# Gate and up products of six SwiGLU layers by Strassen's seven products, with two weight sums formed by DMA

## The chip, the cores and the metric

The kernel runs on one core of a Trainium2 chip, in one launch. The metric is the device time of one execution in microseconds (us). The core has TensorE (PE, with its weight loads listed apart as PEld), VectorE (DVE), ScalarE (ACT), GpSimd (POOL) and SyncE (SP), each with an instruction queue of its own, and 16 DMA engines that move data between HBM and the on-chip memory (SBUF). TensorE writes its results into PSUM.

## The reference

Two models of 512 tokens and width 1,024 run one behind the other, two layers each, in float32, with six SwiGLU feed-forward parts (FFN) of inner width 2,816:

```python
def first_block(x, ...):                     # twice (l = 0, 1)
    ...                                      # four kinds of attention, then y
    x = _layernorm(ALPHA * x + y, ln1_g[l], ln1_b[l])
    f = (jax.nn.silu(x @ w_gate[l]) * (x @ w_up[l])) @ w_down[l]
    x = _layernorm(ALPHA * x + f, ln2_g[l], ln2_b[l])

def swiglu(h, w_gate, w_up, w_down):
    return (jax.nn.silu(h @ w_gate) * (h @ w_up)) @ w_down

def second_block(x, ...):                    # twice (l = 0, 1)
    x = x + 0.5 * swiglu(rms_norm(x, ffn_norm[l, 0]), ...)
    ...                                      # sparse attention, RWKV, gated delta rule
    x = x + 0.5 * swiglu(rms_norm(x, ffn_norm[l, 1]), ...)
```

The six FFNs are called FFN1 to FFN6 here, in the order in which they run: FFN1 and FFN2 belong to the first model, FFN3 (layer 0, first), FFN4 (layer 0, second), FFN5 and FFN6 to the second.

## The kernel before

Activations lie transposed: eight tiles `x[k]` of 128 channels by 512 tokens. Every matrix product is computed to nearly float32 accuracy from halves: an operand is cast to a rounded part `h` (ACT) and the rest `l` is a subtraction (DVE), and one product is three matmuls, h·h, h·l and l·h, which add up in PSUM (`mm3`, which calls `mm`, L164).

An FFN works on 22 "f tiles" of 128 of the 2,816 inner columns. For one f tile, gate and up take 2 (gate, up) x 8 (k tiles) x 3 = 48 matmuls with 512 columns of tokens. Their weights come by `weight` (L222 and after): one DMA of 128x1024 (512 KB) on SP's queue into a raw tile (tag "wr", three of them), the cast `gh` or `uh` on ACT (L235), and the subtraction `gl` or `ul` on DVE (L236), into tags "wh" and "wl" (three each). The result is taken out of PSUM by silu on ACT (L592, L595) and a multiplication on DVE (`hh`, L597), and split into `hh` and `hl` (L213, L214). Where the input is normalised by rms (FFN3 to FFN6), a factor `rs` per token is multiplied in afterwards (L594 and L599), so the products run on un-normalised tiles.

The 22 f tiles are worked in two halves of 11 (`HALF`): gate and up of 11 f tiles, then the down product of these 11 (eight output tiles of 33 matmuls with 512 columns, weights in pieces of 768 and 640 columns), then the same for the other 11. The down result is added into `x[j]` by DVE (`evac`, given by the caller).

Where an FFN follows a layer norm (FFN1, FFN2, FFN3), its first three (`PRE1`, FFN1 and FFN2) or four (`PRE2`, FFN3) f tiles are "early": their products are taken on the not yet normalised `x` (`presplit`, `psh` and `psl`) with 256-column matmuls `gup` and 258-column matmuls `gux` (`gemmx`, L343), while DVE and ACT work through the layer norm (`ln`, L506 to L520). ACT and DVE copy the results out (`gr`, `ur`, `gw`), and `unfold` (L477 to L479) puts the norm in later.

A tile framework with a scheduler orders the instructions of each engine from their priorities and inserts the semaphores; within one engine the order is then fixed. PSUM has eight banks in tags "s" (four), "o" and "d" (two each).

## Time and profile before

| | |
|---|---|
| time before, median of 3 runs | 3742.06 us (3739.53 to 3742.39) |
| the profiled execution's own time | 3745.34 us |
| its span, first to last instruction | 3743.6 us |
| mean granted TensorE clock | 0.985 |
| busy: PE, PEld, DVE, ACT, POOL | 97 %, 78 %, 56 %, 39 %, 8 % |
| HBM traffic over the span | 85 GB/s |

The profile is one execution. Busy time of PE is the sum of its matmuls as the trace shows them; these are pipelined, so one that lasts 0.39 us is followed by the next one 0.23 us later. How fast a row of matmuls runs is therefore read from start to start ("pitch"), not from the mean duration; the same holds in a smaller measure for DVE and ACT.

### The profile page before, as it was taken

Reading aid. Unit: us, or ns where it says so; the run is one execution under the profiler, and the core shown is the slowest. Engines: PE = TensorE matmul, PEld = TensorE weight load, DVE = VectorE, ACT = ScalarE, POOL = GpSimd, SP = SyncE. Lnnn points to the kernel's source line nnn. Section 1 sums busy time; section 2 is a strip of 40 time slices with the busy share of each in tenths; the row PEclk is TensorE's granted clock in tenths of the full one; section 3 lists DMA queues with packets and bytes.
Section 4 is the critical chain, followed back from the end, with each engine's and each line's share of the span. In section 5 each row is a group of like instructions: output and inputs, shape, how many; then the busy total and the mean of one; then the engine's idle time right before and its main releaser. Section 6 shows DMA issues by size and latency. Waiting matters only on the chain.

```text
span 3743.6 us, 48619 instructions
## 1 busy us (share of the span) xinstructions
PE 3644.6 (97%) x18628; PEld 2936.3 (78%) x18628; DVE 2103.4 (56%) x4405; ACT 1443.8 (39%) x2706; POOL 289.8 (8%) x294
## 2 busy tenths in 40 slices
PE   9999999899999999999998999999999999799999
PEld 7678888776788888888786878888888777688887
DVE  5378334637753357345799564444444678865343
ACT  5455222546442235223443542233223433543222
POOL 1111000111200000001212000000000211100000
PEclk9999999999999999999998999999999999899999
DMA  3113232221223222324212132323233321213232
GB/s 129 47 60 101 85 103 88 92 67 49 89 89 103 87 93 89 103 88 142 81 56 64 40 105 86 101 89 102 84 103 100 95 70 50 80 38 104 92 98 87
DMA packets 146840, 320.67 MB, mean 86 GB/s; under 512 B 31496, under 2 KB 57768, under 8 KB 146352
## 3 DMA queue, kind: packets, MB, share of 16 engines
q1 hardware_dynamic: 146608, 317.57, 26.8%
...
## 4 chain that ended last, share of the span: by engine, by line
PE 88%; DVE 9%; ACT 1%; issue 1%; DMA 1%; POOL 0%; DVEq 0%; ACTq 0%; POOLq 0%
PE gup L164 37%; PE dn L164 19%; PE pjp L164 7%; PE wop L164 4%; PE tp L164 3%; PE sc L164 2%; PE ot L164 1%; PE pt L168 1%; PE gux L164 1%; PE iY L164 1%; PE iR L164 1%; PE G L164 1%; PE rowp L164 1%; PE sb L164 1%; DVE isc L1775 1%
## 5 line engine op out<-in xcount | busy, mean ns | idle before, releaser
L164 PE MATMUL dn<-hh,downl 128*128 128x512 f32 x1056 | 416.2, 394 | 0.0
L164 PE MATMUL dn<-hh,downh 128*128 128x512 f32 x1056 | 416.0, 394 | 0.0
L164 PE MATMUL dn<-hl,downh 128*128 128x512 f32 x1056 | 415.8, 394 | 0.0
L164 PE MATMUL gup<-xsh,gh 128*128 128x512 f32 x976 | 384.7, 394 | 0.6 <-ACT xsh L216 0.6
L164 PE MATMUL gup<-xsl,gh 128*128 128x512 f32 x976 | 384.8, 394 | 0.0
L164 PE MATMUL gup<-xsh,gl 128*128 128x512 f32 x976 | 384.5, 394 | 0.0
L164 PE MATMUL gup<-xsh,ul 128*128 128x512 f32 x976 | 384.5, 394 | 0.0
L164 PE MATMUL gup<-xsh,uh 128*128 128x512 f32 x976 | 384.3, 394 | 0.0
L164 PE MATMUL gup<-xsl,uh 128*128 128x512 f32 x976 | 384.1, 394 | 0.0
L235 ACT CAST downh<-down 128x768 fp32r<-128x768 f32 x192 | 150.1, 782 | 517.9 <-PE dn L164 318.6
L597 DVE TENSOR_TENSOR hh<-gup,silu 128x512 f32<-128x512 f32 x122 | 84.4, 692 | 398.0 <-PE gup L164 392.5
L235 ACT CAST gh<-g 128x1024 fp32r<-128x1024 f32 (+1 forms) x138 | 139.3, 1014 | 412.2 <-issue 324.9
L236 DVE TENSOR_TENSOR downl<-down,downh 128x768 fp32r<-128x768 f32 x192 | 171.8, 895 | 216.7 <-ACT downh L235 216.7
L235 ACT CAST uh<-u 128x1024 fp32r<-128x1024 f32 (+1 forms) x138 | 139.5, 1014 | 353.6 <-PE gup L164 313.7
L236 DVE TENSOR_TENSOR ul<-u,uh 128x1024 fp32r<-128x1024 f32 (+1 forms) x138 | 162.4, 1178 | 151.4 <-ACT uh L235 149.4
L164 PEld LDWEIGHTS dn<-hl,downh 128*128 128x128 f32 x1056 | 198.3, 188 | 46.7
L164 PEld LDWEIGHTS dn<-hh,downl 128*128 128x128 f32 x1056 | 198.3, 188 | 46.6
L164 PEld LDWEIGHTS dn<-hh,downh 128*128 128x128 f32 x1056 | 198.3, 188 | 46.4
L164 PEld LDWEIGHTS gup<-xsh,gh 128*128 128x128 f32 x976 | 183.2, 188 | 44.2 <-ACT xsh L216 1.9
L164 PEld LDWEIGHTS gup<-xsl,gh 128*128 128x128 f32 x976 | 183.2, 188 | 43.6 <-DVE xsl L520 0.6
L164 PEld LDWEIGHTS gup<-xsl,uh 128*128 128x128 f32 x976 | 183.2, 188 | 43.0
L164 PEld LDWEIGHTS gup<-xsh,ul 128*128 128x128 f32 x976 | 183.3, 188 | 42.7
(595 smaller groups left out, 7411.2 us busy)
## 6 DMA issues: line engine op xcount, KB each, us to landing
g<-in_w_gu_dram SPq DMA_DIRECT2D x132, 512.0 KB, 3.5
u<-in_w_gu_dram SPq DMA_DIRECT2D x132, 512.0 KB, 3.5
...
pj<-in_w_in_dram SPq DMA_DIRECT2D x62, 512.0 KB, 3.6
...
wo<-in_w_o_dram SPq DMA_DIRECT2D x96, 128.0 KB, 2.2
xd<-x SPq DMA_DIRECT2D x24, 256.0 KB, 2.0
x<-xd SPq DMA_DIRECT2D x24, 256.0 KB, 4.7
```

The source lines that it names most:

```text
L164: self.nc.tensor.matmul(out, l, r, start=start, stop=stop)
L168: self.nc.tensor.transpose(out, src, self.ident if ident is None else ident)
L235: nc.scalar.copy(hi, r)
L236: (eng or nc.vector).tensor_sub(lo, r, hi.bitcast(F32))
L597: nc.vector.tensor_mul(hh, u, s)
L1775: nc.vector.match_replace(acc, m8, acc, -2.0 * BIG)
```

## The change

For f tiles 4 to 21 of every FFN (18 of 22, nine pairs), gate and up are no longer computed as 48 matmuls of 512 columns for each f tile. The two f tiles of a pair are stacked, and the product is seen as a 2x2 by 2x2 block product: gate and up are the two rows, the two halves of the 1,024 channels the inner index (blocks a, b of gate; c, d of up), and the two halves of 256 tokens the columns. Strassen's method, in the form with few additions, computes this from seven block products instead of eight. Each of the seven is 2 (f tiles) x 4 (k tiles) x 3 = 24 matmuls with 256 columns.

The weights of the seven are a, e = c+d, e+a, b, a+c, e+b (with e already holding c+d+a) and d, each split anew into h and l (ACT cast L646, DVE subtraction L647 of the changed kernel). Two of the sums are made by the DMA engines: POOL issues a DMA that adds a block from HBM onto a tile in SBUF (`accum_op`, L621), for e = c+d and for a+c; two are additions on DVE (L640, L642). A pair so takes six DMAs of 512 KB, and the seven products' results are put together by copies on ACT and additions on DVE that read PSUM. Weights are prepared two products ahead (`SAHEAD`), in five raw tiles (`NRAW`) and one of the old ones for b.

The sums of the tokens' side are made once for each FFN (`combos`): for each of four k, seven DVE operations of 256 columns and two of 512, three ACT operations of 256 and two casts of 512, and two more ACT operations where a gain is multiplied in.

The FFN is worked in three chunks (`CHUNKS`): gate and up of f tiles 4 to 11 and their down product, then 12 to 15 with the first four, then 16 to 21. The first four f tiles are now early ones in FFN1 to FFN3 (`PRE1` goes from 3 to 4), and direct 512-column ones in FFN4 to FFN6 (`PRE0`); all are copied out raw, and their silu, split and norm (`later`) run during the first down product. The down weights are repacked: 24 DMAs of 1,024 or 768 columns for an FFN instead of 32, and x is added to 24 times instead of 16. Quarter and half tiles of the mixing part now share their place in SBUF with the raw weight tiles (`phase`), and `presplit` makes its two small copies on ACT (L481, L482) instead of another engine.

```diff
-HALF = 11
+CHUNKS = ((4, 5, 6, 7, 8, 9, 10, 11), (12, 13, 14, 15, 0, 1, 2, 3), (16, 17, 18, 19, 20, 21))
+NRAW = 5
+SAHEAD = 2
 BIG = 1.0e30
 ALPHA = 4.0 ** 0.25
 SLOT = 520
 NWR = 3
 NWS = 3
 HEAD = 1
-PRE1 = 3
+PRE1 = 4
 PRE2 = 4
+PRE0 = 4
...
+    def combos(self, x, gcol, out):
...
+        for k in range(KT // 2):
+            p, q = x[k], x[k + KT // 2]
+            if gcol is not None:
+                g = []
+                for j, v in ((k, p), (k + KT // 2, q)):
+                    g.append(self.S("xg"))
+                    nc.scalar.activation(g[-1], v, AF.Copy, scale=gcol[:, j:j + 1])
+                p, q = g
+            nh, nl, g = self.S("cnh", F32R), self.S("cnl", F32R), self.S("cg", F32R)
+            t, u = self.S("ct"), self.S("cu")
+            nc.scalar.activation(nh[:, A], p[:, A], AF.Copy, scale=-1.0)
+            nc.scalar.activation(nh[:, B], q[:, B], AF.Copy, scale=-1.0)
+            nc.scalar.copy(g[:, A], q[:, A])
+            nc.vector.tensor_sub(t[:, A], p[:, B], p[:, A])
+            nc.vector.tensor_sub(t[:, B], q[:, B], t[:, A])
+            yield
+            nc.vector.tensor_sub(u[:, A], p[:, B], q[:, B])
+            nc.vector.tensor_sub(u[:, B], q[:, A], t[:, B])
+            hl = []
+            for v in (t, u):
+                hl.append((self.S("cth", F32R), self.S("ctl", F32R)))
+                nc.scalar.copy(hl[-1][0], v)
+            for v, r in ((p, A), (q, B)):
+                nc.vector.scalar_tensor_tensor(nl[:, r], v[:, r], -1.0, nh[:, r].bitcast(F32), op0=OP.mult, op1=OP.subtract)
+            nc.vector.tensor_sub(g[:, B], q[:, A], g[:, A].bitcast(F32))
+            for v, (h, l) in zip((t, u), hl):
+                nc.vector.tensor_sub(l, v, h.bitcast(F32))
+            for m, (h, l) in enumerate(((nh[:, A], nl[:, A]), (hl[0][0][:, A], hl[0][1][:, A]), (hl[0][0][:, B], hl[0][1][:, B]),
+                                        (g[:, A], g[:, B]), (hl[1][0][:, A], hl[1][1][:, A]), (nh[:, B], nl[:, B]),
+                                        (hl[1][0][:, B], hl[1][1][:, B]))):
+                out[m].append((h, l))
+            yield
...
+        def move(i, q, t, add=False):
+            g, h = quarter[q]
+            f = f0 + 2 * i
+            src = wgu[g, f:f + 2, :, h * 512:h * 512 + 512].rearrange("f p c -> p f c")
+            if add:
+                nc.gpsimd.dma_start(t.rearrange("p (f c) -> p f c", f=2), src, accum_op=OP.add)
+            else:
+                nc.sync.dma_start(t.rearrange("p (f c) -> p f c", f=2), src)
...
+        def prep(j):
+            i, s = divmod(j, 7)
+            R = lambda q: raws[i, q]
+            if s == 0:
+                if i == 0:
+                    load(0, "e", "c")
+                    move(0, "d", R("e"), True)
+                    load(0, "a")
+                load(i, "d")
+                load(i, "b")
+            elif s == 2:
+                nc.vector.tensor_add(R("e"), R("e"), R("a"))
+            elif s == 5:
+                nc.vector.tensor_add(R("e"), R("e"), R("b"))
+                del raws[i, "b"]
+            r = R("aeebaed"[s])
+            hi, lo = (tile_(self.wp, "w" + t, NWS, F32R) for t in "hl")
+            nc.scalar.copy(hi, r)
+            nc.vector.tensor_sub(lo, r, hi.bitcast(F32))
+            ws[j] = hi, lo
+            if s == 2:
+                move(i, "c", R("a"), True)
+            if s == 4 and i + 1 < n // 2:
+                load(i + 1, "e", "c")
+                move(i + 1, "d", raws[i + 1, "e"], True)
+                load(i + 1, "a")
+            if s >= 4:
+                del raws[i, "aed"[s - 4]]
...
+        for j in range(total):
+            i, s = divmod(j, 7)
+            if j + SAHEAD < total:
+                prep(j + SAHEAD)
+            between(j)
...
+            for e in range(2):
+                for k in range(H):
+                    w = slice(e * 512 + k * 128, e * 512 + k * 128 + 128)
+                    x, first, last = cs[s][k], fresh and k == 0, k == H - 1
+                    self.mm(a[e], hi[:, w], x[0], first, False, not fresh)
+                    self.mm(a[e], hi[:, w], x[1], False, False, not fresh)
+                    self.mm(a[e], lo[:, w], x[0], False, last, not fresh)
+            A, B = slice(0, 256), slice(256, 512)
+            for e in range(2):
+                if s == 0:
+                    g[e] = self.S("gt")
+                    nc.scalar.copy(g[e][:, A], a[e])
+                elif s == 1:
+                    if e == 0:
+                        u = self.S("up")
+                        u2 = {0: u[:, A], 1: u[:, B]}
+                    nc.scalar.copy(u2[e], a[e])
+                elif s == 2:
+                    nc.scalar.copy(g[e][:, B], a[e])
+                elif s == 3:
+                    nc.vector.tensor_sub(g[e][:, A], a[e], g[e][:, A])
+                elif s == 4:
+                    nc.vector.tensor_add(u2[e], a[e], u2[e])
+                elif s == 5:
+                    nc.vector.scalar_tensor_tensor(g[e][:, B], a[e], -1.0, g[e][:, B], op0=OP.mult, op1=OP.subtract)
+                    if rows() is not None:
+                        nc.vector.tensor_mul(g[e], g[e], rows())
+                    nc.scalar.activation(g[e], g[e], AF.Silu)
+                else:
+                    put(f0 + 2 * i + e, g[e], a[e], u2[e])
...
+        def put(f, s, ua, ub):
+            nc.vector.tensor_mul(s[:, 0:256], ua, s[:, 0:256])
+            nc.vector.tensor_mul(s[:, 256:512], ub, s[:, 256:512])
+            if stats is not None:
+                nc.vector.tensor_mul(s, s, rows)
+            h[f] = self.split(s, "h")
...
-                    gu = raw.pop(0)
+            if finish:
+                raw.append(early(f, xs))
+                if f == 1:
+                    lnr = rows
+                    todo = finish(lnr, cs)
+            else:
+                raw.append([(self.evac(ps, "a", name="gu"[i] + "r"), None) for i, ps in enumerate(products(f, xs))])
...
+            new = [f for f in fs if f >= npre]
+            self.fast(wgu, new[0], len(new), cs, lambda: rows if stats is not None else None, put, between)
+            last = n == len(CHUNKS) - 1
+            if last:
+                self.phase("M")
+                cs = None
             for j in range(KT):
-                if half and ahead and j == KT - 3:
+                if last and ahead and j == KT - 3:
                     ahead()
                 acc = self.P("dn", "do"[j % 2])
-                for a, b in ((0, 6), (6, HALF)):
-                    w = self.weight(wdn[half, j, :, a * 128:b * 128], b - a, 128, "down")
-                    for f in range(a, b):
-                        self.mm3(acc, w[f - a], h[o + f], f == 0, f == HALF - 1)
-                evac(half, j, acc)
+                w = self.weight(wdn[j, :, o * 128:(o + len(fs)) * 128], len(fs), 128, "down")
+                for i, f in enumerate(fs):
+                    self.mm3(acc, w[i], h[f], i == 0, i == len(fs) - 1)
+                evac(n == 0, last, j, acc)
+                if n == 0:
+                    next(rest, None)
+            for f in fs:
+                h[f] = None
+            o += len(fs)
 
 
```

Three places show how the order of instructions moves. The first is DVE in FFN1, where the layer norm ends. Before, its last additions (L506, L507) and the subtractions `xsl` that the direct products read (L520) stand among the early tiles' multiplications (L477, `ur`) and the weights' splits (L236):

```order
L506 TENSOR_TENSOR lnt_858_3499<-x_512_2030,lnr_813_3204 128x512
L520 TENSOR_TENSOR xsl_844_3375<-x_510_2026,xsh_843_3374 128x512
L507 TENSOR_TENSOR lnt_858_3499<-lnt_858_3499,lnb_814_3205 128x512 [waits DVE_49]
L506 TENSOR_TENSOR lnt_861_3507<-x_513_2032,lnr_813_3204 128x512
L236 TENSOR_TENSOR gl_883_3606<-g_881_3603,gh_882_3605 128x1024 [waits DMAHW5_49,Activation_49]
L507 TENSOR_TENSOR lnt_861_3507<-lnt_861_3507,lnb_814_3205 128x512 [waits DVE_49]
L520 TENSOR_TENSOR xsl_860_3504<-x_511_2028,xsh_859_3503 128x512 [waits Activation_49]
L506 TENSOR_TENSOR lnt_864_3515<-x_514_2034,lnr_813_3204 128x512
L520 TENSOR_TENSOR xsl_863_3512<-x_512_2030,xsh_862_3511 128x512 [waits Activation_49]
L507 TENSOR_TENSOR lnt_864_3515<-lnt_864_3515,lnb_814_3205 128x512 [waits DVE_49]
L477 TENSOR_TENSOR ur_856_3494<-ur_856_3494,lnr_813_3204 128x512
```

Now the layer norm is over before these rows; `gw` (L369) copies from the PSUM tile `gux` of the fourth early f tile, `ur` (L492) is that tile's multiplication, and the rows L584 to L597 are `combos` of the first k, with the split of the third product's weights (`swwl`, L647) among them:

```order
L492 TENSOR_TENSOR gr_857_3554<-gr_857_3554,lnr_815_3211 128x512
L369 COPY gw_861_3609<-gux_859_3559 128x2 [waits Activation_49]
L492 TENSOR_TENSOR ur_860_3608<-ur_860_3608,lnr_815_3211 128x512
L584 TENSOR_TENSOR ct_865_3616<-x_508_2023 128x256
L587 TENSOR_TENSOR cu_866_3617<-x_508_2023,x_512_2031 128x256
L585 TENSOR_TENSOR ct_865_3616<-x_512_2031,ct_865_3616 128x256 [waits DVE_49]
L595 TENSOR_TENSOR cg_864_3615<-x_512_2031,cg_864_3615 128x256 [waits Activation_49]
L588 TENSOR_TENSOR cu_866_3617<-x_512_2031,ct_865_3616 128x256 [waits DVE_49]
L647 TENSOR_TENSOR swwl_907_3724<-swwr2_898_3705,swwh_906_3723 128x1024 [waits Activation_49]
L594 SCALAR_TENSOR_TENSOR cnl_863_3614<-x_508_2023,cnh_862_3613 128x256
L594 SCALAR_TENSOR_TENSOR cnl_863_3614<-x_512_2031,cnh_862_3613 128x256
L597 TENSOR_TENSOR ctl_868_3626<-ct_865_3616,cth_867_3625 128x512 [waits Activation_49]
```

So the whole of `combos`, four groups like this, now stands behind a copy of the last early tile, where before there was no such sum. The second place is PE at the same point of FFN1. Before, direct products of 512 columns follow the last early matmul there. Now the last early matmul is followed by the first two of the seven products, on `cnh`, `cnl`, `cth`, `ctl` from `combos`, and these two are taken in turn k by k:

```order
L179 MATMUL gux_859_3559<-psh_794_3049,ul_844_3379 128x258
L179 MATMUL gup_908_3728<-cnh_862_3613,swwh_902_3714 128x256 [waits Activation_49]
L179 MATMUL gup_909_3729<-cnh_862_3613,swwh_902_3714 128x256
L179 MATMUL gup_914_3762<-cth_867_3625,swwh_904_3718 128x256 [waits Activation_49]
L179 MATMUL gup_915_3763<-cth_867_3625,swwh_904_3718 128x256
L179 MATMUL gup_908_3728<-cnl_863_3614,swwh_902_3714 128x256 [waits DVE_49]
L179 MATMUL gup_908_3728<-cnh_862_3613,swwl_903_3715 128x256
L179 MATMUL gup_909_3729<-cnl_863_3614,swwh_902_3714 128x256
L179 MATMUL gup_909_3729<-cnh_862_3613,swwl_903_3715 128x256
L179 MATMUL gup_914_3762<-ctl_868_3626,swwh_904_3718 128x256 [waits DVE_49]
```

Each k of the first two products waits for its own sums. The third place is DVE in the middle of gate and up in an FFN with rms factors. Before, one f tile is these six rows:

```order
L594 TENSOR_TENSOR silu_4240_19527<-gup_4238_19477,rs_4179_19165 128x512 [waits PE_49]
L236 TENSOR_TENSOR ul_4249_19546<-u_4247_19543,uh_4248_19545 128x1024 [waits DMAHW5_49,Activation_49]
L597 TENSOR_TENSOR hh_4241_19530<-gup_4239_19478,silu_4240_19527 128x512 [waits PE_49,Activation_49]
L599 TENSOR_TENSOR hh_4241_19530<-hh_4241_19530,rs_4179_19165 128x512 [waits DVE_49]
L236 TENSOR_TENSOR gl_4258_19612<-g_4256_19609,gh_4257_19611 128x1024 [waits DMAHW6_49,Activation_49]
L214 TENSOR_TENSOR hl_4243_19534<-hh_4241_19530,hh_4242_19533 128x512 [waits Activation_49]
```

Now this stands at the border of two pairs in FFN6 (`gt` and `up` hold the pair's gate and up, `swwr2_6971` is e of the next pair, `swwr_6980` its b):

```order
L647 TENSOR_TENSOR swwl_6984_36402<-swwr2_6971_36269,swwh_6983_36401 128x1024 [waits DMASW7_49,Activation_49]
L761 TENSOR_TENSOR gt_6962_36228<-gup_6960_36202,gt_6962_36228 128x256 [waits PE_49,Activation_49]
L762 TENSOR_TENSOR gt_6962_36228<-up_6968_36262,gt_6962_36228 128x256
L761 TENSOR_TENSOR gt_6963_36230<-gup_6961_36203,gt_6963_36230 128x256 [waits PE_49,Activation_49]
L764 TENSOR_TENSOR gt_6962_36228<-gt_6962_36228,rs_6607_33833 128x512 [waits DVE_49]
L762 TENSOR_TENSOR gt_6963_36230<-up_6968_36262,gt_6963_36230 128x256
L640 TENSOR_TENSOR swwr2_6971_36269<-swwr2_6971_36269,swwr2_6972_36272 128x1024
L229 TENSOR_TENSOR hl_6986_36433<-gt_6962_36228,hh_6985_36432 128x512 [waits Activation_49]
L764 TENSOR_TENSOR gt_6963_36230<-gt_6963_36230,rs_6607_33833 128x512 [waits DVE_49]
L647 TENSOR_TENSOR swwl_6990_36445<-swwr2_6971_36269,swwh_6989_36444 128x1024 [waits Activation_49]
```

The sum e+a (L640) and the split of it (the `swwl` that reads `swwr2_6971` again) stand behind five of the finished pair's operations. On POOL's queue, which had no DMA at this place, stand the adding DMAs, two for each pair; in FFN1 (`swwr2_899` is a of the first pair, `swwr2_950` e of the third pair):

```order
L621 DMA swwr2_899_3708<-in_w_gu1_dram 128x2x512 [waits DVE_49,Activation_49]
L621 DMA swwr2_950_4038<-in_w_gu1_dram 128x2x512 [waits DMAHW7_49,DMASW0_49,DVE_49]
L621 DMA swwr2_920_3798<-in_w_gu1_dram 128x2x512 [waits DMAHW2_49,DVE_49,Activation_49]
L621 DMA swwr2_981_4281<-in_w_gu1_dram 128x2x512 [waits DMAHW3_49,DMASW1_49,DVE_49]
```

The first of these waits for DVE (the sum e+a) and ACT (the cast of a) before it may add c onto a.

## Rows read from the trace of the kernel before

**Rows 1.** the page's head and its busy time by engine (us, share, instructions)

```profile
span 3743.6 us, 48619 instructions
PE 3644.6 (97%) x18628; PEld 2936.3 (78%) x18628; DVE 2103.4 (56%) x4405; ACT 1443.8 (39%) x2706; POOL 289.8 (8%) x294
```

**Rows 2.** the page's chain that ended last, by engine and by line

```profile
PE 88%; DVE 9%; ACT 1%; issue 1%; DMA 1%; POOL 0%; DVEq 0%; ACTq 0%; POOLq 0%
PE gup L164 37%; PE dn L164 19%; PE pjp L164 7%; PE wop L164 4%; PE tp L164 3%; PE sc L164 2%; PE ot L164 1%; PE pt L168 1%; PE gux L164 1%; PE iY L164 1%; PE iR L164 1%; PE G L164 1%; PE rowp L164 1%; PE sb L164 1%; DVE isc L1775 1%
```

**Rows 3.** the page's costliest groups: line, engine, operation, shapes, count, busy us, mean ns, idle

```profile
L164 PE MATMUL gup<-xsh,gh 128*128 128x512 f32 x976 | 384.7, 394 | 0.6 <-ACT xsh L216 0.6
...
L164 PEld LDWEIGHTS gup<-xsh,gh 128*128 128x128 f32 x976 | 183.2, 188 | 44.2 <-ACT xsh L216 1.9
```

**Rows 4.** windows in the first and fifth FFN: us, busy per engine, granted clock, DMA share, GB/s

```profile
496.08:618.46 122.38, 122.38 (x528) 98.90 (x527) 39.74 (x43) 33.73 (x43) 0.00 (x0) 1.00 0.30 92
...
2604.00:2664.00 60.00, 60.00 (x262) 48.94 (x261) 27.11 (x32) 17.87 (x22) 0.00 (x0) 1.00 0.29 90
```

**Rows 5.** timeline of PE in the first FFN, direct products: start, duration

```profile
379.99 0.39 PE L164 MATMUL gup<-xsh,gh 128*128 128x512 f32 x1
...
383.00 0.40 PE L164 MATMUL gup<-xsl,gh 128*128 128x512 f32 x1
```

**Rows 6.** timeline of PE in the early tiles of the first FFN

```profile
309.58 0.28 PE L164 MATMUL gux<-psl,gh 128*128 128x258 f32 x1
...
311.48 0.29 PE L164 MATMUL gux<-psh,gl 128*128 128x258 f32 x1
```

**Rows 7.** the same timeline, 6 us earlier, after an idle of PE

```profile
303.02 0.39 PE L164 MATMUL gup<-psl,gh 128*128 128x256 f32 x1 [0.64 <-DVE psl L469]
...
304.34 0.42 PE L164 MATMUL gux<-psl,uh 128*128 128x258 f32 x1
...
306.90 0.41 PE L164 MATMUL wop<-mxh,wol 128*128 128x512 f32 x1
307.14 0.39 PE L164 MATMUL wop<-mxh,woh 128*128 128x512 f32 x1
```

**Rows 8.** DVE's groups by form: count, busy us, mean ns, idle before and what ended it

```profile
L236 DVE TENSOR_TENSOR gl<-g,gh 128x1024 fp32r<-128x1024 f32 x126 | 155.0, 1230 | 9.1 <-ACT gh L235 5.6
...
L214 DVE TENSOR_TENSOR hl<-hh,hh 128x512 fp32r<-128x512 f32 x132 | 90.6, 686 | 22.0 <-ACT hh L213 22.0
...
L597 DVE TENSOR_TENSOR hh<-gup,silu 128x512 f32<-128x512 f32 x122 | 84.4, 692 | 398.0 <-PE gup L164 392.5 <-ACT silu L595 3.9 <-ACT silu L592 1.4
```

**Rows 9.** timeline of DVE in the first FFN's early part: copies of 256 out of PSUM

```profile
334.34 0.42 DVE L196 COPY ur<-gux 128x256 f32<-128x256 f32 x1
334.68 0.15 DVE L354 COPY gw<-gux 128x2 f32<-128x2 f32 x1
```

**Rows 10.** timeline of DVE a little later: 1,024 columns, then 512

```profile
337.15 1.22 DVE L236 TENSOR_TENSOR gl<-g,gh 128x1024 fp32r<-128x1024 f32 x1
338.29 0.69 DVE L506 TENSOR_TENSOR lnt<-x,lnr 128x512 f32<-128x512 f32 x1
338.89 0.69 DVE L520 TENSOR_TENSOR xsl<-x,xsh 128x512 fp32r<-128x512 f32 x1
```

**Rows 11.** ACT's groups by form

```profile
L235 ACT CAST gh<-g 128x1024 fp32r<-128x1024 f32 x126 | 132.5, 1052 | 411.4 <-issue 324.9 <-PE dn L164 41.3 <-PE gup L164 41.2
...
L194 ACT COPY pT<-pt 128x256 f32<-128x256 f32 x36 | 12.7, 371 | 12.3 <-PE pt L168 11.7 <-PE ot L164 0.2
```

**Rows 12.** the page's DMA issues: count, KB each, us from issue to landing

```profile
g<-in_w_gu_dram SPq DMA_DIRECT2D x132, 512.0 KB, 3.5
...
wo<-in_w_o_dram SPq DMA_DIRECT2D x96, 128.0 KB, 2.2
...
x<-xd SPq DMA_DIRECT2D x24, 256.0 KB, 4.7
```

**Rows 13.** the page's DMA queues: packets, MB, share of 16 engines

```profile
q1 hardware_dynamic: 146608, 317.57, 26.8%
```

151 lines of the change are left out of this document (97 added, 54 removed).

## The prediction

> **What bounds the kernel now.** I read the head of the page first: PE is busy 97 % of the span, DVE, ACT and POOL far less [rows 1]. The chain that ended last says the same of the path: 88 % of it is PE, and the gate and up products `gup` alone are 37 % [rows 2]; PE hardly waits for them, 0.6 us over 976 matmuls of one kind [rows 3]. So here a matmul less is time less, as long as nothing else becomes late. Then I asked in windows what the other engines have to spare in gate and up: in 122.38 us with 528 matmuls DVE is busy 39.74, ACT 33.73, POOL nothing, the DMA engines 30 %; with rms factors DVE has 27.11 of 60 us [rows 4]. Last I read the pitch of matmuls, from start to start: 122.38/528 = 0.2318 us for 512 columns, and 3.01/13 = 0.2315 in the timeline [rows 4, 5]; for about 256 columns, each with a weight load of its own, 1.90/16 = 0.119 us [rows 6].
>
> **The matmuls.** Of the 5,856 direct matmuls (six kinds of 976 [rows 3]), those of f tiles 4 to 21 change: 18 x 48 x 6 = 5,184, by 0.2318 us 1201.6 us. In their place come 54 pairs of 168 matmuls with 256 columns: 9,072 by 0.119 us, 1079.6 us. That is 2.26 us a pair (22.25 before, 19.99 after), together -122.0 us. Two f tiles more are early ones: 96 matmuls of 256 or 258 columns, 11.4 us, for 48 direct, 11.1: +0.6 for both. Net -121.4 us. The saving is an eighth of the gate and up work, less what 0.119 is above half of 0.2318.
>
> The row shows 0.119 us from start to start while a weight load is listed with 188 ns [rows 3, 6]: the load lies beside the matmuls before it. [...]
>
> **DVE and ACT for a pair, beside these 20 us.** DVE: seven splits and two additions of 1,024 columns by 1.14 us (337.15 to 338.29), ten operations of 256 that read PSUM by 0.34, two `hl` of 512 by 0.60 [rows 9, 10]: 10.3 + 3.4 + 1.2 = 14.9 us. With rms factors (FFN3 to FFN6, 36 pairs) four more of 512: 17.3 us, 87 % of the pair; by the durations in the groups (1.23, 0.42, 0.69 [rows 8, 9]) it would be 19.4 us. ACT: seven casts by 1.05, six copies by 0.37, two silus and two casts of 512 at about 0.6 (between the rows for 1,024 and 256) [rows 11]: 12.0 us. So PE still is the longest, but on DVE an order matters. Its cover is thin, where before PE's end was what it waited for (398 us of idle before `hh` [rows 8]).
>
> Where it is thinnest: with T0 the end of a pair's seventh product, DVE does L761, L762, L761, L764, L762 and then e+a (L640): 4 x 0.34 + 0.60 + 1.14, with the wait at the start, T0+3.4. Two operations of 512 stand behind it and lie beside the cast on ACT; the split is done at about T0+5.8. PE needs it when it is through the next two products: 48 x 0.119 = 5.7, and 0.24 later for the first l·h, T0+5.95. That is 0.1 to 0.2 us of slack, with waits between engines not counted. Bounds: nothing, or 1 us if each of some five handovers costs 0.2; times 36 pairs 0 to 36. I take 0.2 us, 7 us, near the lower end, since the pitch rows already hold DVE's own issue. The pairs of FFN1 and FFN2 have 0.6 us more and cost nothing.
>
> **The adding DMAs.** POOL issues two for each pair, where DMAs before ran only in the hardware queue beside a few instruction loads [rows 13]; no row shows one, nor an issue from POOL. c+d is wanted some 14 us after its issue and lies beside PE. a+c is the tight one: it may start when e+a is done (T0+3.4), and the fifth product starts at T0+4x2.86 = T0+11.4. Before that come the cast, 1.05, and the split, 1.23, which may end 0.24 later: it has to land within 11.4+0.24-3.4-1.05-1.23 = 6.0 us. What stands behind it: on ACT and DVE, whose queues are in order, the cast and split of this product block the copies and sums behind them, so a late landing stops PE by its whole excess in each of 54 pairs. The landing time: a plain 512 KB takes 3.5 us, 128 KB 2.2 [rows 12], so 0.34 us for 100 KB on a fixed 1.8; twice the bytes give 5.2, and twice the whole row 7.0. Ends: 3.5 us (cost 0; an earlier landing gives nothing back) and 7.0 us (1.0 x 54 = 54 us). I take 5.2, since both the tile and HBM must be read but the fixed part is paid once: cost 0. Traffic goes from 92 GB/s [rows 4] to 6 x 0.524 MB / 20 us = 157 GB/s, at 30 % busy DMA engines now no bound.
>
> [...]
>
> **The sums of the tokens' side.** In FFN1 to FFN3 the order puts them behind the copy from the last early f tile. With E the end of that tile on PE: evacuation and `ur` take until E+1.75; four k by 7 x 0.34 + 2 x 0.60 = 3.58 us [rows 9, 10] are 14.3; the split of the third product's weights and e+b stand among them, 2.3; the last subtraction, 0.6, is not wanted yet: E+17.7. PE does the first two products k by k beside it; four matmuls are left, so they end at E+18.2 instead of E+5.7: 12.5 us lost. [...] FFN3 has the rms steps between: 16. Together 44.4 us. (Lower bound 30, if the k groups run at PE's side without a clock drop and DVE's rows for 256 are shorter out of SBUF; upper 60, at durations instead of pitch.) Before, the layer norm lay wholly beside the early tiles. In FFN4 to FFN6 the sums stand beside four direct tiles, 44.5 us of PE; in the order only the last k, the third split and e+b come after them: cast and wait 1.3, split 1.2, addition 1.1, sums 3.0, last matmuls 0.5, 7.1 against 5.7 us of PE, with waits 2 us, and 1 for the clock: 3 each, 9 us.
>
> **Borders and the rest.** Before each down product the last pair's `h` is ready about T0+3.5 and T0+5.5; PE has down matmuls of the other f tiles to do (528 in an FFN, as before). Only the third chunk with its six f tiles and the second with rms factors leave about 1 us: 6 us. At the start of an FFN, SP's first load waits until the shared tiles are free, and POOL's first add waits for c with splits (`wol`) behind it: 0 to 2 us each, I take 5 together. The silu of the first tiles lies beside the first down product (DVE there as in [rows 4], about half free): 0. Eight more additions to x per FFN: also there, 0.
>
> **The sum.** -121.4 + 7 + 0 + 44.4 + 9 + 6 + 5 = -50.0 us. From the profiled execution's 3745.3 (its span and 1.7 us around it) that is 3695.3; the median shown is 0.09 % lower, 3742.06/3745.34, so 3692.
>
> **Rivals.**
> 1. *The adding DMA lands late.* For it: no row for it, POOL must issue it, and 6.0 us is little against 3.5 for a plain one; 256 KB rows took 4.7 us elsewhere [rows 12]. Against: c's and a's bytes are 0.5 MB on engines that are 70 % free. Price 54 us for each us above 6.0: it eats the gain at 6.9 us; at 8 us +108, 3800; at 10 us 3908. This is the case on the other side.
> 2. *DVE becomes the bound* where rms factors stand: 19.4 us by durations, and with handovers a pair takes 21 to 22 us instead of 20. 36 pairs by 1 to 2 us: 3728 to 3764. Against: DVE rows follow each other at their pitch when data is there [rows 10].
> 3. *256 columns don't keep 0.119* in long rows with so many weight loads: at 0.1245 the gain is gone, at 0.188 (the load's duration) +626, 4318. Against: sixteen in a row, and early tiles throughout [rows 6].
> 4. *The starts cost less* (30 for the first three, nothing for the last, no thin spot): 3660.
>
> **How the numbers follow.** The forecast 0.50, all of it faster. Rival 1 0.25 (0.20 slower, 0.03 the same, 0.02 faster), rival 2 0.17 (0.08, 0.06 the same, 0.03 slower), rival 3 0.01 (slower), rival 4 0.07 (faster). Within 0.2 % (7.5 us), what a measurement of this kernel can tell from no change, is "the same". So faster 0.67, the same 0.09, slower 0.24. The forecast's own range is 3660 to 3720, by its bounds (starts 30 to 60, thin spot 0 to 36); for 8 in 10 I leave out a late landing above 8 us and take 3645 to 3795.
>
> **What would show it.** In gate and up of FFN1 a pitch of 0.119 and 168 matmuls in 20.0 us show the first term. An adding DMA's time from issue to landing, below or above 6.0 us, and PE's wait at the fifth product for ACT's cast of `swwr2`, decide rival 1. PE's wait at the third product for `swwl`, in FFN3 to FFN6 only, and DVE without idle there, decide rival 2. At the start of FFN1 to FFN3 PE should wait 12 to 14 us for `cth`, `cnl` and `ctl`, in pieces, with the granted clock below 1; in FFN4 to FFN6 about 3. If those starts show no wait, or pairs take over 20.5 us, the forecast is wrong.

## The result, and the profile after

The changed kernel takes 3697.88 us (median of four, 3696.66 to 3712.78), the one before 3742.22 beside it: ratio 0.9888, 95 % interval 0.986 to 0.9916, 44 us or 1.1 % less. The profile is of the execution that took 3712.78 us, 15 us more than the other three, so places in it are compared, and totals are taken from the medians. First the head of its page and the chain [rows 1, 2]:

```profile
span 3711.0 us, 58410 instructions
...
PE 3561.6 (96%) x22612; PEld 3059.9 (82%) x22612; DVE 2611.0 (70%) x5227; ACT 1772.7 (48%) x3392; POOL 422.7 (11%) x402
...
PE 74%; DVE 16%; DMA 3%; ACT 3%; issue 3%; POOL 0%; ACTq 0%; POOLq 0%; DVEq 0%; SPq 0%
PE gup L179 25%; PE dn L179 19%; PE pjp L179 6%; PE tp L179 3%; PE wop L179 3%; PE sc L179 2%; DVE swwl L647 2%; PE gux L179 2%; PE ot L179 1%; DMA swwr<-in_w_gu_dram 1%; ACT swwh L646 1%; PE pt L183 1%; PE iY L179 1%; PE G L179 1%; PE iR L179 1%
```

DVE does a quarter more, and the chain has moved: `gup` fell from 37 % to 25 %, DVE rose from 9 % to 16 %, and the weights' splits (`swwl`) and DMAs into `swwr` appear on it. PE is still the bound, but no longer alone. Groups of the same page [rows 3, 8]:

```profile
L647 DVE TENSOR_TENSOR swwl<-swwr,swwh 128x1024 fp32r<-128x1024 f32 x378 | 460.9, 1224 | 222.5 <-ACT swwh L646 214.3
L179 PE MATMUL gup<-cth,swwh 128*128 128x256 f32 x1728 | 487.4, 284 | 21.6 <-ACT cth L592 17.3
...
L179 PEld LDWEIGHTS gup<-cth,swwh 128*128 128x128 f32 x1728 | 326.5, 190 | 25.9 <-ACT cth L592 20.6
L621 POOL DMA_DIRECT2D swwr<-in_w_gu_dram x108 | 130.0, 1203 | 1862.5 <-DVE swwr L640 1068.1
```

PE waits 17.3 us for the casts of the sums (`cth`), where it waited 0.6 in the direct products. Where the gain lies is read from windows over FFN1, FFN2 with FFN3, FFN4 with FFN5, and FFN6 (columns as in [rows 4]), of before and then of after:

```profile
292.00:680.20 388.20, 384.63 (x1797) 316.68 (x1798) 184.83 (x277) 135.78 (x190) 20.37 (x15) 1.00 0.31 95
984.00:1746.40 762.40, 757.64 (x3621) 628.19 (x3622) 380.40 (x560) 265.97 (x371) 20.46 (x15) 1.00 0.31 96
2173.80:2920.50 746.70, 745.67 (x3237) 605.02 (x3236) 337.44 (x445) 225.26 (x299) 5.94 (x9) 1.00 0.31 99
3362.00:3739.70 377.70, 377.47 (x1636) 305.45 (x1634) 163.06 (x213) 107.08 (x140) 3.20 (x3) 1.00 0.30 96
```

```profile
298.50:681.60 383.10, 370.30 (x2494) 339.04 (x2493) 268.26 (x387) 185.21 (x313) 40.77 (x31) 0.99 0.43 112
984.40:1744.20 759.80, 735.25 (x4966) 675.61 (x4966) 544.64 (x812) 369.01 (x597) 67.13 (x55) 0.98 0.44 116
2175.60:2896.10 720.50, 711.92 (x4532) 639.00 (x4532) 514.32 (x750) 341.09 (x517) 48.59 (x43) 1.00 0.46 123
3339.60:3706.90 367.30, 361.19 (x2284) 323.73 (x2282) 252.66 (x366) 164.86 (x249) 22.45 (x19) 1.00 0.43 114
```

FFN1 to FFN3 together gain 5.1 + 2.6 = 7.7 us, FFN4 to FFN6 26.2 + 10.4 = 36.6. (That these make 44.3, as the medians do, is chance: the two profiled spans differ by 32.6 us, so outside these windows this execution of the changed kernel was 11.7 us longer.) With a layer norm ahead, a saving of some 20 us an FFN is nearly used up at the start. Windows of the changed kernel: the start of FFN1's seven products, then two whole pairs without rms factors, two with, and three with:

```profile
366.00:383.80 17.80, 10.18 (x48) 8.16 (x48) 17.13 (x40) 10.63 (x24) 0.00 (x0) 0.81 0.21 29
503.80:543.50 39.70, 39.70 (x337) 39.67 (x336) 28.58 (x38) 21.30 (x32) 3.61 (x3) 1.00 0.63 159
2362.20:2402.50 40.30, 39.98 (x337) 39.78 (x336) 31.55 (x43) 21.54 (x32) 3.61 (x3) 1.00 0.61 156
2447.10:2508.00 60.90, 60.26 (x506) 59.80 (x506) 49.45 (x70) 32.14 (x49) 4.82 (x4) 1.00 0.49 118
```

The pitch is 39.70/337 = 0.118 us, a pair 19.85 us; with rms factors 20.15 and 20.3. PE's waits for the weights' splits in the whole execution (total us, count, longest):

```profile
PE gup L179 <- DVE swwl L647: 11.0, 30, 0.6
```

At the start of FFN1's seven products 48 matmuls (5.7 us at the pitch) take 17.8, DVE is busy 17.13 of them, and the clock stands at 0.81. PE's timeline there, with its waits in brackets:

```profile
366.42 0.51 PE L179 MATMUL gup<-cnh,swwh 128*128 128x256 f32 x2 [0.42 <-ACT cnh L581]
369.13 0.50 PE L179 MATMUL gup<-cth,swwh 128*128 128x256 f32 x2 [2.20 <-ACT cth L592]
...
374.95 0.80 PE L179 MATMUL gup<-cth,swwh 128*128 128x256 f32 x2 [1.74 <-ACT cth L592]
375.55 0.41 PE L179 MATMUL gup<-cnl,swwh 128*128 128x256 f32 x1
375.76 0.41 PE L179 MATMUL gup<-cnh,swwl 128*128 128x256 f32 x1
...
378.51 0.51 PE L179 MATMUL gup<-cth,swwh 128*128 128x256 f32 x2 [0.61 <-ACT cth L592]
```

and DVE beside it, the first and the last sum:

```profile
367.34 0.42 DVE L584 TENSOR_TENSOR ct<-x 128x256 f32<-128x256 f32 x1
...
383.22 0.68 DVE L597 TENSOR_TENSOR ctl<-cu,cth 128x512 fp32r<-128x512 f32 x1
```

DVE works from 367.34 to 383.90 us without a pause, each k of PE waits for its cast, and after a wait matmuls follow each other at 0.21 us (375.55, 375.76), at a granted clock of 0.50 from 374.95 to 376.50. Last the DMA issues and the new queue [rows 12, 13]:

```profile
q0 software_dynamic: 29376, 56.63, 9.7%
...
swwr<-in_w_gu_dram SPq DMA_DIRECT2D x216, 512.0 KB, 4.0
swwr<-in_w_gu_dram POOLq DMA_DIRECT2D x108, 512.0 KB, 6.2
```

An adding DMA lands 6.2 us after its issue (median), a plain one of the same size 4.0.

### The profile page after: what moved, and what is told of

The parts are those of the page before. It is cut to its first block, busy times and chain, and to the rows that moved or that the text cites. A ratio compares the mean times of both kernels' runs of the same rounds, so it can differ in the third digit from the quotient of the medians.

```text
span 3711.0 us, 58410 instructions
## 1 busy us (share of the span) xinstructions
PE 3561.6 (96%) x22612; PEld 3059.9 (82%) x22612; DVE 2611.0 (70%) x5227; ACT 1772.7 (48%) x3392; POOL 422.7 (11%) x402
## 3 DMA queue, kind: packets, MB, share of 16 engines
q0 software_dynamic: 29376, 56.63, 9.7%
## 4 chain that ended last, share of the span: by engine, by line
PE 74%; DVE 16%; DMA 3%; ACT 3%; issue 3%; POOL 0%; ACTq 0%; POOLq 0%; DVEq 0%; SPq 0%
PE gup L179 25%; PE dn L179 19%; PE pjp L179 6%; PE tp L179 3%; PE wop L179 3%; PE sc L179 2%; DVE swwl L647 2%; PE gux L179 2%; PE ot L179 1%; DMA swwr<-in_w_gu_dram 1%; ACT swwh L646 1%; PE pt L183 1%; PE iY L179 1%; PE G L179 1%; PE iR L179 1%
## 5 line engine op out<-in xcount | busy, mean ns | idle before, releaser
L646 ACT CAST swwh<-swwr 128x1024 fp32r<-128x1024 f32 x378 | 395.0, 1051 | 510.5 <-PE gup L179 205.3
L647 DVE TENSOR_TENSOR swwl<-swwr,swwh 128x1024 fp32r<-128x1024 f32 x378 | 460.9, 1224 | 222.5 <-ACT swwh L646 214.3
L179 PE MATMUL gup<-cth,swwh 128*128 128x256 f32 x1728 | 487.4, 284 | 21.6 <-ACT cth L592 17.3
L179 PE MATMUL gup<-cth,swwl 128*128 128x256 f32 x1728 | 488.9, 283 | 2.3 <-DVE swwl L647 2.2
L179 PE MATMUL gup<-ctl,swwh 128*128 128x256 f32 x1728 | 489.2, 283 | 1.6 <-DVE ctl L597 1.6
L179 PEld LDWEIGHTS gup<-cth,swwh 128*128 128x128 f32 x1728 | 326.5, 190 | 25.9 <-ACT cth L592 20.6
L621 POOL DMA_DIRECT2D swwr<-in_w_gu_dram x108 | 130.0, 1203 | 1862.5 <-DVE swwr L640 1068.1
L179 PEld LDWEIGHTS gup<-ctl,swwh 128*128 128x128 f32 x1728 | 328.8, 190 | 3.8 <-DVE ctl L597 3.8
L179 PEld LDWEIGHTS gup<-cth,swwl 128*128 128x128 f32 x1728 | 328.6, 190 | 3.7 <-DVE swwl L647 3.7
L179 PE MATMUL gup<-cnl,swwh 128*128 128x256 f32 x864 | 244.6, 284 | 3.0 <-DVE cnl L594 3.0
L179 PE MATMUL gup<-cnh,swwl 128*128 128x256 f32 x864 | 243.5, 282 | 0.0
L179 PE MATMUL pjp<-xsh,pjh 128*128 128x512 f32 x472 | 202.2, 429 | 14.2 <-ACT tpe L218 8.0
```

Of the source, the lines that this page charges most:

```text
L179: self.nc.tensor.matmul(out, l, r, start=start, stop=stop, skip_group_check=more)
L621: nc.gpsimd.dma_start(t.rearrange("p (f c) -> p f c", f=2), src, accum_op=OP.add)
L646: nc.scalar.copy(hi, r)
L647: nc.vector.tensor_sub(lo, r, hi.bitcast(F32))
```

## The experiments

Ratios are to the kernel before on the same chip, with the 95 % interval. "Per pair" is the time from the first to the last matmul of a chunk's seven products, over its pairs; the loss of a start is what a chunk needs beyond 0.119 us a matmul. Both are read from the timeline of one execution, the profiled one, while the ratios are of all executions.

**What the parts bring.** `again` is the changed kernel once more.

> The changed kernel once more, for a second profile. Theory: its first profiled execution (3712.78 us) was a long one, and the median of the runs, 3697.9, comes again within 4 us; pairs take 19.9 us without and 20.2 us with rms factors, the first chunks of FFN1 to FFN3 lose 13 us each, those of FFN4 to FFN6 3 to 7 us. On one point two views differ: in the first profile the early tiles of FFN1 began at 298.5 us where they began at 292.1 before. If the loads of the first pair, which stand on SP's queue ahead of the projection's weights, cause this, it comes again (296 to 299); if it was that execution, the early tiles begin at 291 to 294.

Measured 0.9887 (0.9871 to 0.9903), 3702.09 us. Its early tiles began at 290.6 and not at 298.5, so that delay belonged to the first profiled execution. FFN6's window (3335.90 to 3699.30) is 363.4, not 367.3. The starts differ too: the first chunks of FFN1 to FFN3 lose 15.9, 14.6 and 13.7 us, where the first profile has 12.7, 13.0 and 13.7, and those of FFN4 to FFN6 5.0, 3.4 and 4.5 instead of 6.9, 3.4 and 6.8. The first two products of FFN1 in `again`, the same 48 matmuls in the same order as above:

```profile
356.90:374.70 17.80, 11.61 (x48) 10.31 (x48) 17.23 (x40) 10.17 (x22) 0.00 (x0) 0.62 0.16 28
```

The granted clock is 0.62 here and was 0.81 there. So between two executions of one kernel a first chunk moves by up to 3 us, and a smaller difference between two runs' chunks shows nothing by itself.

`chunks_direct` keeps the chunks, the silu in the first down product and the repacked down weights, but works f tiles 4 to 21 directly (the lines that bring back the split inputs are left out here):

```diff
...
-            self.fast(wgu, new[0], len(new), cs, lambda: rows if stats is not None else None, put, between)
+            for f in new:
+                hidden(f, *products(f, xs))
```

> Strassen alone undone: f tiles 4 to 21 by direct products of 512 columns as before, everything else as changed (three chunks, first tiles' silu in the first down product, four early tiles, tiles shared). Theory (the rest of the change is neutral): within 6 us of before, 3738 to 3748, so that the products with their sums make the whole difference. Rival (the three chunks or the later silu give or cost something by themselves): more than 8 us off.

Measured 1.001 (0.9999 to 1.002). The rest of the change is worth nothing within the interval; the gain is that of the seven products with their sums.

**The rms factors.** `no_rows` leaves out both multiplications in a pair:

```diff
-            if stats is not None:
-                nc.vector.tensor_mul(s, s, rows)
...
-            self.fast(wgu, new[0], len(new), cs, lambda: rows if stats is not None else None, put, between)
+            self.fast(wgu, new[0], len(new), cs, lambda: None, put, between)
```

> The four multiplications of 512 columns by the rms factor are left out of every pair of FFN3 to FFN6 (the output then lacks this factor there). Theory (the 0.25 us that such pairs take more come from DVE's longer row at the border of pairs): they fall to 19.9 us, and the time by 36 x 0.25 = 9 us and up to 5 us more at the first chunks: 3684 to 3690. Rival (they come from waits of another kind, the landing of a+c or the order of the splits): less than 4 us.

Measured 0.9828 (0.9809 to 0.9846): 22 us less than `again` on the same chip. Three pairs of FFN4, as in the window above:

```profile
2427.80:2487.30 59.50, 59.50 (x505) 59.50 (x504) 44.16 (x60) 32.59 (x50) 4.81 (x4) 1.00 0.50 123
```

PE is without a gap, and DVE does 44.16 us where it did 49.45. Of PE's 30 waits for the splits five are left:

```profile
PE gup L179 <- DVE swwl L647: 2.0, 5, 0.5
```

The first chunks of FFN4 to FFN6 go from 21.7, 20.9, 21.7 a pair (21.2, 20.8, 21.1 in `again`) to 20.5, 20.3, 20.4. `rows_late` keeps the result: the second factor is applied to the down product's eight results of each chunk instead of to every f tile:

```diff
...
-            if stats is not None:
-                nc.vector.tensor_mul(s, s, rows)
...
+                if stats is not None:
+                    t = self.S("dnr")
+                    nc.vector.tensor_mul(t, acc, rows)
+                    acc = t
```

> The second multiplication by the rms factor leaves the pairs (L764, L757) and is done on the down product's results instead: one more operation of 512 columns from PSUM at each of 24 additions to x in FFN3 to FFN6. Theory (DVE's row at the border of pairs is too long by a few tenths of a us, DVE has room in the down products): pairs with factors fall from 20.2 to 19.95, first chunks of FFN4 to FFN6 lose 2 us less, in all 10 to 14 us: 3684 to 3690. Rival (DVE is late by the other multiplication or by the wait for the adding DMA): 0 to 4 us. A third view (the longer chain from down product to x delays the parts after it): slower by 5 us or more.

Measured 0.9849 (0.9834 to 0.9864), 3683.72 us, 14 less than the changed kernel and the fastest version here that leaves nothing out. Steady pairs go at 19.8, though DVE does more in all (2625.3 us busy, 2612.5 in `again`).

**The adding DMAs.** `dve_sums` has none: plain loads of a, b, c, d, and both sums on DVE, a+c as (c+d+a)-d:

```diff
-                    move(0, "d", R("e"), True)
...
+            elif s == 1:
+                nc.vector.tensor_add(R("e"), R("e"), R("d"))
...
+            elif s == 4:
+                nc.vector.tensor_sub(R("a"), R("e"), R("d"))
...
-            if s == 2:
-                move(i, "c", R("a"), True)
...
-                move(i + 1, "d", raws[i + 1, "e"], True)
```

> No adding DMAs: c+d is added on DVE, and a+c is formed on DVE as (c+d+a)-d; four loads of 512 KB for a pair instead of six transfers. DVE has two more operations of 1,024 columns, 2.3 us a pair: 17.2 us without and 19.6 us with rms factors, of 20. Theory (DVE is at its edge and the adding DMAs keep it from being the bound): pairs without factors stay at 19.9, pairs with factors take 20.6 to 21.5 us: 15 to 50 us slower, 3713 to 3748. Rival (the landing of the adding DMA, 6.2 us, is what holds pairs up): pairs with factors get no longer, the PE wait of 1.7 us at the first border of FFN4 to FFN6 goes, and the time falls by 5 to 15 us.

Measured 0.989 (0.9875 to 0.9905), the same as `again`. Three pairs of FFN4:

```profile
2432.30:2493.70 61.40, 59.86 (x505) 59.44 (x503) 53.87 (x73) 32.41 (x49) 0.00 (x0) 1.00 0.28 85
```

DVE does 4.4 us more in three pairs, and the pairs take 0.2 us longer each. PE's waits for the splits (L650 here) double:

```profile
PE gup L179 <- DVE swwl L650: 22.9, 27, 1.5
```

All pairs together take 1149.3 us, 10.6 more than in `again`, and the rest of this execution 10.7 less; why the rest is shorter is not shown. So DVE's additions cost a little in the pairs, far from the 15 to 50 us expected, and the sums by DMA bring nothing that the time shows. `plain_loads` makes the adding DMAs plain ones in SP's queue, so that two of the weight sums lack a part:

```diff
-                nc.gpsimd.dma_start(t.rearrange("p (f c) -> p f c", f=2), src, accum_op=OP.add)
+                nc.sync.dma_start(t.rearrange("p (f c) -> p f c", f=2), src)
```

> The two adding DMAs of each pair become plain loads on SP's queue into the same tiles (the sums c+d and a+c then lack one part). Same bytes over the wire, no add, no POOL. Theory (a landing of 6.2 us is just in time; it holds up PE only at the first border of FFN4 to FFN6, 1.7 us and a stretch at the lower clock): first chunks of FFN4 to FFN6 2 to 3 us shorter, the rest within 0.05 us a pair: 6 to 10 us less, 3690 to 3696. Rival (each landing costs): pairs with rms factors fall from 20.2 to 19.9: 20 us less.

Measured 0.9877 (0.9861 to 0.9894), within the intervals of the changed kernel. The first chunks of FFN4 and FFN6 fall to 20.9 a pair, 0.2 to 0.8 under the two executions of the changed kernel, FFN5's stays at 20.9; later pairs with factors rise to 20.2 to 20.7. What the adding DMA's later landing costs is a few us at most, and the time shows nothing of it.

**The starts.** `one_k` makes the sums of one k only and uses them for all four:

```diff
-        for k in range(KT // 2):
+        for k in range(1):
...
-                out[m].append((h, l))
+                out[m] += [(h, l)] * (KT // 2)
```

> Only the sums of the first k are made and used for all four (the output lacks the others' tokens): a quarter of the sums, nothing else changed. Theory (what the starts lose is these sums): first chunks of FFN1 to FFN3 lose 2 to 4 us instead of 13, those of FFN4 to FFN6 1 to 2 us less: 30 to 36 us less, 3664 to 3672. Rival (the starts wait for weights, PSUM or the norm): first chunks still lose 8 us or more.

Measured 0.9819 (0.9797 to 0.984). PE's waits in this kernel:

```profile
PE gup L179 <- ACT cth L592: 6.3, 3, 2.2
```

Three of the 14 waits are left, and the first chunks of FFN1 to FFN3 lose 6.4, 5.4 and 7.7 us instead of 12.7 to 15.9, but not the 2 to 4 expected. What is left may be the first k, which nothing hides, and its clock; no run separates it. The other runs keep all sums and move them. `early_sums` emits them before the last early tile, and in FFN4 to FFN6 twice as fast:

```diff
-                end, v = steps(todo, 100 if f == npre - 1 else LSTEP if finish else 2)
...
+                end, v = steps(todo, (100 if f >= npre - 2 else LSTEP) if finish else 4)
...
```

> The sums of the tokens' side are emitted ahead of the last early tile in FFN1 to FFN3, and within the first two direct tiles in FFN4 to FFN6. Theory (the loss at the start is the place of these sums in DVE's order, behind the last early tile's copy): the first chunk of FFN1 to FFN3 loses 2 to 5 us instead of 13, that of FFN4 to FFN6 1 to 2 us less, in all 25 to 35 us: 3663 to 3673. Rival (the sums wait for room or for the norm, not for their place): the first chunks lose 10 us or more as before, and the time stays within 8 us of 3698. A third view: the last early tile's multiplications, now behind the sums, keep weights or PSUM from PE: half of the gain, 3680 to 3690.

Measured 0.9872 (0.9852 to 0.9891). FFN1 to FFN3 have 24.2, 24.1, 25.1 a pair in the first chunk (23.2, 23.2, 23.4 in the changed kernel; 24.0, 23.6, 23.4 in `again`). But the scheduler put the first products ahead of part of the last early tile's up product, so 24 of its matmuls, 2.9 us at the pitch, now run within the chunk. From the first early matmul to the chunk's last one FFN1 and FFN2 take 159.7 and 159.0 us, where the changed kernel takes 160.6 and 160.9 (162.2 and 162.6 in `again`), FFN3 152.2 where it took 150.5 (149.2): hardly anything gained in two FFNs, 2 to 3 us lost in the third, and PE still waited for the sums. FFN4 to FFN6 fell to 20.8, 20.3, 20.8. `mid_sums` emits them between that tile's gate and up part:

```diff
...
-                raw.append(early(f, xs))
+                raw.append(early(f, xs, sums if f == npre - 1 else None))
...
-                end, v = steps(todo, 100 if f == npre - 1 else LSTEP if finish else 2)
...
+                end, v = steps(todo, LSTEP if finish else 4)
...
```

> The rest of the layer norm and all sums of the tokens' side are emitted between the gate and the up part of the last early tile, and that tile's gate is copied out ahead of them; in FFN4 to FFN6 they are emitted with the first two direct tiles. In the kernel with early sums PE's order had the first two products in front of the last early tile's up part, which waited for ACT's copy of its gate; here the early matmuls stand first again. Theory (the sums cost what of them lies behind the last early matmul): first chunks of FFN1 to FFN3 lose 4 to 8 us instead of 13, 15 to 27 us in all, and 5 more in FFN4 to FFN6: 3672 to 3682. Rival (sums take a fixed stretch of DVE and ACT after the norm, wherever they stand): 3692 to 3700 as with early sums.

Measured 0.9884 (0.9869 to 0.9899); FFN1 23.3, FFN2 23.2, FFN3 24.1. In FFN1 the last sum ends 14 us after the early tile instead of 18, and the loss, 13.3 us, lies between the 12.7 and 15.9 of the changed kernel's two executions. The window of its start in FFN1:

```profile
358.00:380.00 22.00, 15.37 (x81) 13.71 (x81) 17.92 (x36) 10.64 (x23) 1.20 (x1) 0.69 0.23 48
```

The granted clock is 0.69; over the same length from the first product on, the changed kernel has 0.84 in one execution and 0.61 in the other. So no gain of the earlier sums is shown, and what became of the 4 us stays open. `mid_need` also changes their order: for all k what the first product reads, then the second, and so on (`need` in place of `combos`):

```diff
...
-            yield from self.combos(x, None, cs)
+            yield from self.need(x, None, cs)
...
```

> The sums of the tokens' side in the order in which the seven products need them: for all four k first the negated halves (first product), then the differences (second and third), then the fourth product's, then the rest; emitted where the kernel with the sums in the middle of the last early tile has them (FFN1 to FFN3), and with the first two direct tiles in FFN4 to FFN6. Theory (the first two products were taken k by k and each k waited for a whole group of sums, and PE's clock fell in those waits): in FFN1 and FFN2 the first product stands ready when the early tiles end, the second at 8 us after it; the first chunk loses 4 to 6 us instead of 13, and the time is 3668 to 3680. Rival (the DVE work of sums and splits as a whole is what PE waits for, in whatever order): the loss only moves to the fifth product, first chunks lose 10 us or more, 3690 to 3698.

Measured 0.9916 (0.9903 to 0.993), slower than the changed kernel; FFN1 to FFN3 lose 18.6, 17.8 and 24.3 us. The first product ran without a wait and the second with waits for `cth`; then PE waited for a PSUM tile:

```profile
PE gup L179 <- ACT ur L794: 20.2, 3, 8.3
```

ACT's copy of the early tile's up part stands behind all the sums in ACT's row. `best` joins `mid_need` and `rows_late`, with no other edit.

> Both together: sums in the order of need in the middle of the last early tile, and the second rms factor on the down product's results. Theory: the gains add, 18 to 30 us and 10 to 14 us against the changed kernel's 3698: 3656 to 3670. Rival (they relieve the same wait at the first chunks of FFN3 to FFN6): 3670 to 3680.

Measured 0.9894 (0.9879 to 0.9909). FFN4 to FFN6 have 19.9, 19.8, 19.8 a pair in the first chunk (20.4, 20.3, 20.2 in `rows_late`): their sums no longer show. Whether the order of need does this or their earlier place, both of which `best` has, is not separated; with all rms factors in the pairs, `mid_need` has 20.8, 20.3, 21.2 there. FFN1 to FFN3 lose as in `mid_need`. `after_tile` is `best` with the sums of FFN1 to FFN3 behind the whole early tile again:

```diff
...
-                raw.append(early(f, xs, sums if f == npre - 1 else None))
+                raw.append(early(f, xs))
...
-                end, v = steps(todo, LSTEP if finish else 4)
+                end, v = steps(todo, 100 if f == npre - 1 else LSTEP if finish else 4)
...
```

> The sums of the tokens' side in order of need (all k for the first product, then for the second, and so on), but in FFN1 to FFN3 emitted behind the whole last early f tile, as in the changed kernel, so that ACT's copies of that tile's results stand ahead of them; in FFN4 to FFN6 within the first two direct tiles, as in the run best; the second rms multiplication at the down product's results, as in rows_late. Theory (the path at the start of FFN1 to FFN3 is which sum is wanted first, and the run best was spoilt by the copies behind the sums alone): the chunk's first product starts about 5 us after the end of the early tile on PE, the second ends 13 us after it, the rest follows at the pitch: 8 to 9 us lost in place of 13, three times; FFN4 to FFN6 at 19.8 to 19.9 us a pair in the first chunk as in best, 6 us under rows_late. Together 3665 to 3672 us. Rival (DVE's and ACT's work on the sums as a whole, and the half clock during the waits, set the loss, in whatever order): FFN1 to FFN3 lose 13 us each still, and only the 6 us of FFN4 to FFN6 come: 3676 to 3680.

Measured 0.9901 (0.9884 to 0.9917): neither view held. FFN1 to FFN3 lose 21 to 22 us each (25.3, 25.3, 25.5 a pair), FFN4 to FFN6 have 19.9, 19.8, 19.9. PE's waits:

```profile
PE gup L179 <- ACT gt L734: 19.3, 3, 6.6
PE gup L179 <- ACT cth L629: 9.1, 12, 2.0
```

The third product adds to the first one's PSUM tile, which ACT must copy first, and that copy (`gt`) stands behind the casts of all seven products' sums. The idea that the order of need alone shortens these starts fell in both forms: each kept the wanted sums early and put something else, which PE waited for, behind the rest. An order with the products' copies between the sums was not tried.

## Why the prediction held

Forecast 3692, measured 3697.88; forecast -50.0, measured -44.3 between the medians. By FFN the sum's terms make, with nine pairs at -20.3 us and a border at 1 us each: FFN1 -4.8, FFN2 and FFN3 -6.4, FFN4 and FFN5 -29.2, FFN6 -14.6, together -55.0. The windows show -5.1, -2.6, -26.2, -10.4, together -44.3 (`again`: -45.8).

**The matmuls** held: 0.118 us from start to start, 19.85 us a pair for 19.99 forecast, 8 us over 54 pairs on the good side. The weight loads of these 9,072 matmuls, listed at 190 ns each, lay beside the matmuls: in the window 503.80:543.50 above PE was busy 39.70 and PEld 39.67 of 39.70 us.

**The starts of FFN1 to FFN3** held in mechanism and size. PE ends the early tile at about 365.7 us and is through the first two products at 383.8, 18.1 us later, forecast 18.2. The first chunks lose 12.7, 13.0 and 13.7 us (15.9, 14.6 and 13.7 in `again`), forecast 14.2, 14.2 and 16. The forecast's 14.2 is 12.5 us lost to the sums and 1.7 for a lower clock, and its 3 us for a start of FFN4 to FFN6 hold 1 us for the clock: no run shows either term by itself. What the runs show in their place: the first chunks of FFN4 to FFN6 had a clock of 0.98, 1.00 and 0.98 in the first profile. Where FFN1's start went at a clock of 0.81, in the first profile, 115 matmuls were listed in its first 26 us; in `again`, where the same order went at 0.62, 100. That is 15 x 0.118 = 1.8 us between two executions of one kernel; the rest of the 3.2 us between their losses lies later in the chunk. No run shows what a start at the full clock would lose, and that 14.2 fell between the two executions is in part luck.

**The thin spot with rms factors** was mis-sized: 7 us forecast, 22 by `no_rows`. The forecast was right about DVE's row but not about which product waits for it. FFN4, from the start of a pair's first product at 2382.07, DVE:

```profile
2382.97 0.68 DVE L764 TENSOR_TENSOR gt<-gt,rs 128x512 f32<-128x512 f32 x1
...
2385.64 0.68 DVE L764 TENSOR_TENSOR gt<-gt,rs 128x512 f32<-128x512 f32 x1
2386.31 2.36 DVE L647 TENSOR_TENSOR swwl<-swwr,swwh 128x1024 fp32r<-128x1024 f32 x2
```

and PE:

```profile
2387.77 0.63 PE L179 MATMUL gup<-cg,swwh 128*128 128x256 f32 x4
2388.72 0.39 PE L179 MATMUL gup<-cg,swwl 128*128 128x256 f32 x1 [0.32 <-DVE swwl L647]
```

The third product's split is done at about 2387.5, 5.4 us in, in time, as forecast (5.8 against 5.95). But the scheduled order lets PE begin the fourth product (`cg`) ahead of the third, and its split is the second of the two in that row, 1.14 us later. Such a border costs about 0.5 us (0.60 from start to start in place of 0.12); six in each of four FFNs make 12 of the 22 us, and most of the rest stands in the first chunks of FFN4 to FFN6, below. So what had to be judged was the slack of the fourth product's split, which the order puts first. This is read from the trace; that a shorter row of DVE removes the wait is what `rows_late` shows, and no run changed PE's order alone.

**The adding DMA** took 6.2 us, not the 5.2 that the author estimated with the bytes doubled (the queue lists 56.63 MB for the 108, 512 KB each; a doubling is not shown), 1.2 of it POOL's own instruction; that is above the limit of 6.0. By rival 1's price this should have cost 0.2 x 54 = 11 us. Steady pairs of FFN1 and FFN2 show nothing of it: the landing then eats what slack there is, and only a place that is late already pays. That is the first border of FFN4 and of FFN6 (FFN5's shows no such wait), here FFN6's; POOL's issue first:

```profile
3417.83 1.20 POOL L621 DMA_DIRECT2D swwr<-in_w_gu_dram  x1 [3.94 <-DVE gt L761]
```

then ACT, then PE:

```profile
3424.01 1.04 ACT L646 CAST swwh<-swwr 128x1024 fp32r<-128x1024 f32 x1 [1.79 <-DMA swwr<-in_w_gu_dram]
3424.96 0.64 ACT L685 COPY gt<-gup 128x256 f32<-128x256 f32 x2
```

```profile
3425.38 0.39 PE L179 MATMUL gup<-cth,swwh 128*128 128x256 f32 x1 [1.65 <-ACT gt L685]
...
3426.42 0.42 PE L179 MATMUL gup<-cth,swwh 128*128 128x256 f32 x1
3426.63 0.41 PE L179 MATMUL gup<-ctl,swwh 128*128 128x256 f32 x1
```

The mechanism is rival 1's: the late cast blocks ACT's copies, PE waits 1.65 us and soon runs at 0.21 us a matmul. But it needs the delays of the rms factors as well: without these the first chunks are at 20.3 to 20.5.

**The starts of FFN4 to FFN6**, forecast at 3 us each, lost 6.9, 3.4 and 6.8 (5.0, 3.4 and 4.5 in `again`) for these causes together; without rms factors 2.5, 1.7 and 2.4 over 19.85 a pair.

**Taken together** all pairs' chunks take 1140.3 us (1138.6 in `again`); the forecast's terms make 54 x 19.99 + 44.4 + 9 + 7 = 1139.9. Errors of +15 (rms), -8 (pitch), -6 and -2 (starts, as `no_rows` has them over 19.85 a pair) cancelled, so an agreement this close is luck. The 10 us by which the windows fall short of the terms (55.0 - 44.3) lie outside the pairs, and only a part was found: in FFN1 the fourth early tile lengthens the early part from 55.0 (292.1 to 347.1) to 67.9 us (298.5 to 366.4), 12.9 where 11.4 was forecast (11.3 in `again`), and FFN2's by 13.0 in both. Borders cost under 6: down products keep 0.2315 us a matmul to within 0.5 us in all but one of 18. Outside the windows, where 5 were forecast, `again` has +5.6 (its span is 40.2 shorter, its windows 45.8), with several us of variation in single stretches; that part too stays open.

**Rivals.** That DVE is the bound fell with `dve_sums`: 108 more additions on it cost 0.2 us a pair and nothing that the time shows. Its sign, PE's waits for the splits, did come, nearly all in FFN3 to FFN6 and at the fourth product, but at 11.0 us in 30 waits, and pairs took 20.3 us, not 21 to 22. That the pitch is lost fell with the windows, that the starts are cheaper with FFN1's rows.
